# New durations in a hand-made order planner, vector products let through earlier, a conformer moved up: a two-layer hybrid diffusion backbone on one Trainium2 core

## The chip, the cores and the metric

One core of a Trainium2 chip runs the whole program. The metric is device time in microseconds, the median of three runs. A core has five engines with a queue of their own each: TensorE (PE) multiplies matrices, VectorE (DVE) and ScalarE (ACT) work on rows, GpSimd (POOL) does some additions, SyncE (SP) issues the DMAs. Each takes its instructions in the order in which the program puts them, and waits at semaphores for the others.

## The reference

Two layers over 256 latent and 256 context tokens of width 1024. In each layer a modulated RMSNorm feeds one wide projection, whose columns go to four mixers; their outputs are projected, gated, summed and projected again; then sixteen experts choose their tokens.

```python
for l in range(2):
    mod = silu(c) @ ada_w[l] + ada_b[l]                  # shifts, scales, gates (also for the context)
    u = modulate(rms_norm(h), mod[0], mod[1])
    z = u @ w_in[l]                                      # diff q,k,v | hyena | conformer | mla q,kv | 4 gates
    y = [diff_attention(z), hyena(z), conformer(z), mla(z)]
    h = h + mod[2] * ((sum(sigmoid(g[i]) * (y[i] @ w_branch[i]) for i in range(4))) @ w_out)
    h = h + mod[5] * expert_choice_ffn(modulate(rms_norm(h), mod[3], mod[4]))   # 16 experts, 32 tokens each
return rms_norm(h_latent)
```

In the second layer only the latent tokens are carried to the end; the context serves as keys and values. Everything is float32; the large products are made from a high and a low part (three matmuls each, `mm3`, lines 355 to 357).

## The kernel before

The program is straight-line: its order on every engine is fixed when it is built. Each piece of work is a Python generator (a worker) that emits instructions and yields what they cost: `{"pe": ..., "dve": ..., "act": ...}`. `Order.run` (line 175) keeps one planned clock per engine. It goes through the list of workers and resumes the first whose ready time is not after the planned TensorE time; if none is ready, the one that is ready soonest, and TensorE's planned time moves there. So the place in the list is the priority. The costs of the row engines come from `_a`, `_d` and `_q` (lines 215 to 225), those of TensorE from constants at the place (0.00042 us a column of a matmul). The planner knows nothing of the PSUM buffers (two `pm`, three `psc`, two `pt`, one `px`); the real waits for them come on the chip.

Layer 0's list begins with the experts' loader, the router and `head`, which cuts the weights of the wide projection into high and low parts (`wq`, ScalarE's cast in line 348, the vector's subtraction in line 349). Then come the modulation products. `body` (line 910), the matmuls of the wide projection, is last: it fills TensorE when nothing else is ready, in pieces of twelve matmuls of 512 columns in layer 0 (256 in layer 1). Its last items are the gates of the four branches, in the order 1, 3, 2, 0 (hyena, latent attention, conformer, differential attention); in layer 0 at most four gate results (`tg`) may be outstanding (`TGMAX`, line 921), in layer 1 ten. `branch` (line 998) multiplies a mixer's output by its weights and by the gate.

The products (`half`, line 500) compute the later shifts, scales and gates on VectorE: a job is one load of 256 KB by SP and, per stream (two in layer 0, one in layer 1), a scalar_tensor_tensor with accumulation (line 521). 96 jobs run in layer 0 and 64 in layer 1. After a job the worker waits until the planned end of its vector work plus `PACE[l]`. When a group is through, a closing worker (`end`) spreads the result as rows (POOL copies, transposes); the first group's are needed by the output projection, which in layer 0 also waits for all products.

The conformer (line 1218) runs 31 taps for each of two halves on VectorE (line 1230), in pairs, then a layer norm through transposes (its last steps are in lines 1260 to 1262). `CP` gives its place: -1 is just above `body`. The latent attention (`mla`, 16 steps in layer 0, 8 in layer 1) and the differential attention (`diff`, as many) go step by step: scores on TensorE, maximum (line 1272) and its negative (1274) on VectorE, exponential (1276) on ScalarE, scaling, transposes, and the product with the values; after a step they wait for the latest planned end plus `LAG[l]`. The differential attention's fourth step waits for the latent attention's end.

`S.wait` (line 249) makes the workers with the overall numbers 41 and 51 wait 0.7 us longer; before, these are the products' row loader of layer 1 and the conformer of layer 1.

```python
PACE, AHEAD = (0.0, -1.5), 2          # 236
CP, RLAG = (-1, -1), 4.0              # 238
S.wait = {41: -0.7, 51: -0.7}         # 249
e = yield {"dve": len(ss) * (_d(512) + 0.07)}   # 524
yield e + PACE[l]                               # 525
gens.insert(CP[l] if CP[l] >= 0 else len(gens) - 1, conformer())   # 1627
```

## Time and profile before

| | us |
|---|---|
| median of 3 runs | 1980.32 (1976.28 to 1982.57) |
| the profiled execution, its own time | 1979.82 |
| its span, first to last instruction | 1978.0 |
| TensorE busy | 1698.5 (86%), mean granted clock 0.913 |
| VectorE busy | 974.6 (49%) |
| ScalarE busy | 461.9 (23%) |
| POOL busy | 220.0 (11%) |
| read from HBM | 547.83 MB |

The span falls into four parts: layer 0's mixers up to about 683 us, its experts up to 1129, layer 1's mixers up to 1514, its experts up to the end. The shares over the span mix these parts; the rows below are taken by stretch. A group of instructions is listed by its source line; `mm3` and `split` are helpers, so that lines 348, 349 and 355 to 357 are told apart by the tiles they write and read. Matmuls are pipelined and their ends are modelled, so a matmul's duration in the trace is longer than the distance between two starts.

### The profile page before, as it was taken

Reading aid. Unit: us, or ns where it says so; the run is one execution under the profiler, and the core shown is the slowest. Engines: PE = TensorE matmul, PEld = TensorE weight load, DVE = VectorE, ACT = ScalarE, POOL = GpSimd, SP = SyncE. Lnnn points to the kernel's source line nnn. Section 1 sums busy time; section 2 is a strip of 40 time slices with the busy share of each in tenths; the row PEclk is TensorE's granted clock in tenths of the full one; section 3 lists DMA queues with packets and bytes.
Section 4 is the critical chain, followed back from the end, with each engine's and each line's share of the span. In section 5 each row is a group of like instructions: output and inputs, shape, how many; then the busy total and the mean of one; then the engine's idle time right before and its main releaser. Section 6 shows DMA issues by size and latency. Waiting matters only on the chain.

```text
span 1978.0 us, 27907 instructions
## 1 busy us (share of the span) xinstructions
PE 1698.5 (86%) x11132; PEld 1106.7 (56%) x11132; DVE 974.6 (49%) x2057; ACT 461.9 (23%) x933; POOL 220.0 (11%) x229
## 2 busy tenths in 40 slices
PE   5899999888989899899999888998997776676675
PEld 2677788666769634433333278887997433322222
DVE  4787789877774312212332285888864111111012
ACT  4423233334332100100100063344442000000001
POOL 1332011031101000000010042320211000000000
PEclk9899999899989899989999998999998877778677
DMA  8525334422345799999999954565759999999997
GB/s 284 170 86 169 128 114 139 145 95 85 111 151 215 267 375 417 419 408 420 419 418 421 404 180 142 172 197 161 220 176 362 417 421 420 420 421 420 421 421 304
DMA packets 185721, 550.71 MB, mean 278 GB/s; under 512 B 13238, under 2 KB 93304, under 8 KB 140408
## 3 DMA queue, kind: packets, MB, share of 16 engines
q1 hardware_dynamic: 185592, 548.94, 72.9%
q8 instruction: 88, 1.44, 0.3%
q14 instruction: 41, 0.34, 0.1%
HBM read 547.83 MB, written 1.05 MB: 277 GB/s over the span
## 4 chain that ended last, share of the span: by engine, by line
PE 50%; DMA 26%; DVE 12%; issue 6%; ACT 4%; POOL 1%; SPq 1%; ACTq 0%; DVEq 0%; POOLq 0%
DMA we<-in_w_ei_dram 14%; PE pm L1965 11%; DMA we<-in_w_eo_dram 9%; PE pm L355 7%; PE pm L357 7%; PE pm L356 7%; PE psc L1990 4%; DVE wq L349 2%; PE psc L1854 2%; PE psc L355 2%; PE psc L357 2%; DVE aw L521 1%; PE psc L356 1%; DMA aw<-in_ada_w_dram 1%; ACT wq L348 1%
## 5 line engine op out<-in xcount | busy, mean ns | idle before, releaser
L1965 PE MATMUL pm<-we,xe 128*32 128x256 f32 (+1 forms) x3040 | 419.4, 543 | 91.0 <-DMA we<-in_w_ei_dram 89.2
L1965 PEld LDWEIGHTS pm<-we,xe 128*32 128x32 f32 (+1 forms) x3040 | 142.1, 137 | 344.6 <-issue 188.6
L355 PE MATMUL pm<-uh,wq 128*128 128x256 f32 (+1 forms) x832 | 291.3, 350 | 2.2 <-ACT u L819 1.9
L356 PE MATMUL pm<-ul,wq 128*128 128x256 f32 (+1 forms) x832 | 281.6, 338 | 1.0 <-POOL ul L828 1.0
L357 PE MATMUL pm<-uh,wq 128*128 128x256 f32 (+1 forms) x832 | 281.3, 338 | 0.0
L1977 DVE SCALAR_TENSOR_TENSOR ea<-ea,pm 128x512 f32<-128x512 f32 (+1 forms) x32 | 17.7, 553 | 420.9 <-ACT ea L1976 420.9
L1990 PE MATMUL psc<-we,eaT 128*32 128x256 f32 (+1 forms) x1440 | 185.2, 509 | 36.7 <-DMA we<-in_w_eo_dram 35.7
L349 DVE TENSOR_TENSOR wq<-wi,wq 128x1024 fp32r<-128x1024 f32 x131 | 166.9, 1285 | 80.3 <-ACT wq L348 79.9
L355 PEld LDWEIGHTS pm<-uh,wq 128*128 128x128 f32 x832 | 161.3, 194 | 23.9 <-issue 5.2
L356 PEld LDWEIGHTS pm<-ul,wq 128*128 128x128 f32 x832 | 161.5, 194 | 17.6 <-POOL ul L828 1.2
L357 PEld LDWEIGHTS pm<-uh,wq 128*128 128x128 f32 x832 | 160.9, 193 | 16.6
L2002 DVE TENSOR_TENSOR ye<-psc,modr 32x512 f32<-32x512 f32 (+1 forms) x120 | 66.4, 553 | 197.0 <-PE psc L1990 195.7
L1990 PEld LDWEIGHTS psc<-we,eaT 128*32 128x32 f32 (+1 forms) x1440 | 64.5, 129 | 151.8 <-issue 81.6
L348 ACT CAST wq<-wi 128x1024 fp32r<-128x1024 f32 x132 | 136.2, 1044 | 11.8 <-DMA wi<-in_w_in_dram 10.4
L1976 ACT ACTIVATE ea<-pm 128x512 f32<-128x512 f32 (+1 forms) x32 | 15.7, 491 | 473.2 <-PE pm L1965 473.2
L1230 DVE SCALAR_TENSOR_TENSOR ca<-up,colt,ca 128x510 f32<-128x510 f32 (+29 forms) x120 | 81.0, 675 | 2.2
L521 DVE SCALAR_TENSOR_TENSOR aw<-aw,h 128x512 f32<-128x512 f32 x96 | 77.5, 807 | 3.4
L2035 ACT COPY eaT<-pt 128x512 f32<-128x512 f32 (+1 forms) x32 | 15.3, 479 | 273.1 <-PE pt L2033 273.1
L1276 ACT ACTIVATE e<-psc,nm 128x512 f32<-128x512 f32 (+1 forms) x72 | 44.4, 617 | 147.7 <-DVE nm L1274 142.8
L355 PE MATMUL pm<-wq,uh 128*128 128x256 f32 (+1 forms) x240 | 72.4, 302 | 4.4 <-DVE rsq L319 1.6
L356 PE MATMUL pm<-wq,uh 128*128 128x256 f32 (+1 forms) x240 | 70.3, 293 | 0.0
L357 PE MATMUL pm<-wq,ul 128*128 128x256 f32 (+1 forms) x240 | 70.2, 293 | 0.0
(407 smaller groups left out, 2603.1 us busy)
## 6 DMA issues: line engine op xcount, KB each, us to landing
we<-in_w_ei_dram SPq DMA_DIRECT2D x241, 1024.0 KB, 19.7
we<-in_w_eo_dram SPq DMA_DIRECT2D x120, 1024.0 KB, 19.8
wi<-in_w_in_dram SPq DMA_DIRECT2D x58, 1024.0 KB, 5.3
aw<-in_ada_t_dram SPq DMA_DIRECT2D x160, 256.0 KB, 5.4
we<-in_w_ei_dram SPq DMA_DIRECT2D x52, 256.0 KB, 8.1
wbr<-in_w_branch_dram SPq DMA_DIRECT2D x40, 256.0 KB, 5.4
wi<-in_w_out_dram SPq DMA_DIRECT2D x8, 1024.0 KB, 5.1
we<-in_w_eo_dram SPq DMA_DIRECT2D x32, 256.0 KB, 5.4
```

Of the source, the lines that this page charges most:

```text
L348: nc.scalar.copy(hi, src)
L349: eng.tensor_tensor(lo, src, hi.bitcast(F32), op=OP.subtract)
L355: nc.tensor.matmul(out, lh, rh, start=first and i == 0, stop=False)
L356: nc.tensor.matmul(out, lh, rl, start=False, stop=False)
L357: nc.tensor.matmul(out, ll, rh, start=False, stop=last and i == n - 1)
L521: nc.vector.scalar_tensor_tensor(o, wt_, 1.0, cb[s, k], op0=OP.mult, op1=OP.mult, accum_out=ends[lm, g][0][:, s, c, k:k + 1])
L1230: nc.vector.scalar_tensor_tensor(o, up[:, :, max(d, 0):256 + min(d, 0)], cw[:, c0 + d:c0 + d + 1], o, op0=OP.mult, op1=OP.add)
L1276: nc.scalar.activation(e, p[:, :nk], AF.Exp, scale=scale, bias=nm, accum_out=s)
L1854: nc.tensor.matmul(p[:, kk * n:(kk + 1) * n], h[2 * s + b][k // 4][:, (k % 4) * 128:(k % 4 + 1) * 128], hot[:, 2 * i + b], start=b == 0, s ...
L1965: nc.tensor.matmul(dst[j * M:(j + 1) * M, :], lhs, w[o + j * FW // 512][:, j * FW % 512:j * FW % 512 + FW], start=k == 0, stop=k == KC - 1 ...
L1990: nc.tensor.matmul(py[j * M:(j + 1) * M, :FW], aT[:, c * 128 + q * M:c * 128 + (q + 1) * M], w[f % 2 * 2 + j * FW // 512][:, j * FW % 512: ...
L2002: nc.vector.tensor_tensor(ye[eg][s][c0 // 512][e4 * CAP:(e4 + 1) * CAP, c0 % 512:c0 % 512 + FW], py[r0:r0 + CAP, :FW], mod5[r0:r0 + CAP, c ...
```

## The change

The planner's constants are replaced: a matmul column 0.000442 us instead of 0.00042, the vector 0.13 + n/915 instead of 0.07 + n/960, POOL 0.15 + n/450 instead of 0.1 + n/480, and 0.1 us (`HOP`) is added to the end of each engine's part of a step before the next engine's part starts. `PACE` of layer 0 goes from 0.0 to -1.5, the value of layer 1. `CP` of layer 1 goes from -1 to 5: the conformer is sixth in layer 1's list of mixers, behind the key rotation and ahead of the products, the query rotation, the differential attention and the branches. All numbers of workers behind it in the list rise by one.

```diff
@@ Order.run
                     e = self.t[k] = max(self.t[k], e) + c
+                    e += HOP
                 best[3] = e
...
+HOP = 0.1
...
 def _d(n):
-    return 0.07 + n / 960
+    return 0.13 + n / 915
 def _q(n):
-    return 0.1 + n / 480
+    return 0.15 + n / 450
...
-    PACE, AHEAD = (0.0, -1.5), 2
+    PACE, AHEAD = (-1.5, -1.5), 2
     PRE, PREW = (1, 3), (1, 3)
-    CP, RLAG = (-1, -1), 4.0
+    CP, RLAG = (-1, 5), 4.0
...
-                                        yield {"pe": 3 * PIECE[l] * step * 0.00042}
+                                        yield {"pe": 3 * PIECE[l] * step * 0.000442}
...
-                            e = yield {"pe": 24 * 0.00042 * w, **cost}
+                            e = yield {"pe": 24 * 0.000442 * w, **cost}
...
-                        e = yield {"pe": 24 * 0.108, "dve": _d(256), "dve " if q == 3 else "pool": _d(256)}
+                        e = yield {"pe": 24 * 0.119, "dve": _d(256), "dve " if q == 3 else "pool": _d(256)}
...
-                    PE = {"pe": nk * 3 * TQ * 0.00042, "dve": _d(TQ)}
+                    PE = {"pe": nk * 3 * TQ * 0.000442, "dve": _d(TQ)}
...
-            MF = 12 * 0.213 * F
+            MF = 12 * 0.226 * F
```

## Rows read from the trace of the kernel before

**Rows 1.** Busy time by stretch: engine, us busy (instructions); clock; DMA share; GB/s.

```profile
core 0: us, PE busy (x) PEld busy (x) DVE busy (x) ACT busy (x) POOL busy (x), PEclk, DMA share, GB/s
...
100.00:216.00 116.00, 109.22 (x558) 88.45 (x557) 96.63 (x188) 32.86 (x61) 26.52 (x24) 0.96 0.37 120
216.00:374.00 158.00, 157.35 (x860) 128.92 (x859) 132.39 (x303) 56.75 (x118) 15.78 (x16) 1.00 0.41 131
374.00:557.00 183.00, 154.05 (x717) 118.40 (x715) 139.92 (x314) 65.56 (x136) 37.46 (x36) 0.92 0.37 119
...
683.00:1129.00 446.00, 422.57 (x1944) 162.56 (x1946) 114.61 (x204) 37.60 (x74) 6.93 (x9) 0.97 1.00 409
...
1160.00:1255.00 95.00, 85.72 (x604) 79.31 (x603) 68.50 (x143) 39.89 (x82) 29.19 (x34) 0.93 0.49 157
...
1300.00:1374.00 74.00, 69.36 (x533) 61.65 (x531) 61.73 (x142) 36.05 (x76) 4.18 (x3) 0.98 0.59 185
1374.00:1452.00 78.00, 74.20 (x604) 73.38 (x604) 59.46 (x111) 37.10 (x64) 15.77 (x18) 0.98 0.60 190
...
1540.00:1965.00 425.00, 295.35 (x3136) 124.64 (x3128) 58.11 (x137) 16.61 (x45) 0.00 (x0) 0.76 1.01 417
```

**Rows 2.** Waits of TensorE, 374 to 609 us: us in total, times, longest.

```profile
PE psc L355 <- ACT wbrh L348: 11.2, 3, 6.7
PE psc L355 <- ACT e L1276: 8.5, 4, 6.2
PE pt L561 <- DVE ol L1522: 4.1, 1, 4.1
```

**Rows 3.** Timeline near 479 us: start, us, instruction, [idle before it, what ended it].

```profile
479.12 0.69 ACT L1276 ACTIVATE e<-psc,nm 128x512 f32<-128x512 f32 x1 [1.26 <-DVE nm L1274]
...
479.95 0.80 PE L355 MATMUL psc<-oh,wbrh 128*128 128x512 f32 x1 [6.24 <-ACT e L1276]
```

**Rows 4.** Line 1418, layer 0: duration ns min/median/max, first and last start.

```profile
L1418 PE MATMUL px<-aT,mv x96: 272/273/324, 251.3 to 368.1; 128*64 128x128 f32 x96
```

**Rows 5.** Timeline: matmuls in a full run, and after a wait.

```profile
480.55 0.63 PE L356 MATMUL psc<-ol,wbrh 128*128 128x512 f32 x1
...
480.97 0.63 PE L357 MATMUL psc<-oh,wbrl 128*128 128x512 f32 x1
...
544.67 0.39 PE L357 MATMUL pm<-uh,wq 128*128 128x512 f32 x1
...
548.75 0.39 PE L357 MATMUL pm<-uh,wq 128*128 128x512 f32 x1
```

**Rows 6.** VectorE's groups, 0 to 1140 us: count, busy us, mean ns, idle before.

```profile
L349 DVE TENSOR_TENSOR wq<-wi,wq 128x1024 fp32r<-128x1024 f32 x66 | 83.5, 1275 | 49.8 <-ACT wq L348 49.7
...
L1272 DVE TENSOR_REDUCE mx<-psc 128x1 f32<-128x512 f32 x24 | 16.4, 682 | 0.7 <-PE psc L1429 0.7
```

**Rows 7.** Line 521, the products, layer 0 and layer 1: ns, first and last start.

```profile
L521 DVE SCALAR_TENSOR_TENSOR aw<-aw,h x96: 691/692/1683, 89.8 to 583.9; 128x512 f32<-128x512 f32 x96
...
L521 DVE SCALAR_TENSOR_TENSOR aw<-aw,cb x64: 674/683/1219, 1175.4 to 1413.4; 128x512 f32<-128x512 f32 x64
```

**Rows 8.** Line 521's busy time in one stretch (products and their accumulator reads).

```profile
374.00:557.00 183.00, 50.19 (x125) 0.92 0.37 119
```

**Rows 9.** The conformer: taps in layer 0, last step in layer 0 and layer 1.

```profile
L1230 DVE SCALAR_TENSOR_TENSOR ca<-up,colt,ca x60: 715/732/1771, 121.8 to 383.8; 128x510 f32<-128x510 f32 x4, 128x508 f32<-128x508 f32 x4, 128x506 f32<-128x506 f32 x4, 128x504 f32<-128x504 f32 x4
...
L1262 DVE SCALAR_TENSOR_TENSOR cx<-cs,cx x2: 691/692/692, 453.6 to 456.5; 128x512 f32<-128x512 f32 x2
...
L1262 DVE SCALAR_TENSOR_TENSOR cx<-cs,cx x2: 424/438/452, 1447.5 to 1449.5; 128x256 f32<-128x256 f32 x2
```

**Rows 10.** Timeline near 421 us: two products and a POOL addition.

```profile
420.48 0.68 DVE L521 SCALAR_TENSOR_TENSOR aj<-aw,h 128x512 f32<-128x512 f32 x1
...
421.20 1.66 DVE L521 SCALAR_TENSOR_TENSOR aw<-aw,h 128x512 f32<-128x512 f32 x1
...
420.64 1.67 POOL L1056 TENSOR_TENSOR acc<-acc,tg 128x512 f32<-128x512 f32 x1 [0.29 <-DVE tg L1054]
```

More of the change, by code (lines that the diff above doesn't have):

```diff
@@ L933, in body @@
                                     if c + step < tn or k < KC - PIECE[l]:
-                                        yield {"pe": 3 * PIECE[l] * step * 0.00042}
+                                        yield {"pe": 3 * PIECE[l] * step * 0.000442}
                             done(j, m)
                             cost = fn(p[:, :tn], evs[m])
-                            e = yield {"pe": 3 * PIECE[l] * step * 0.00042, **cost}
+                            e = yield {"pe": 3 * PIECE[l] * step * 0.000442, **cost}
                             evs[m][0].t = e
```

## The prediction

> **What bounds the kernel now.** I read the busy time by stretch first [rows 1]. In the two expert stretches, 683 to 1129 us and 1540 to 1965 us, the DMA engines are busy the whole time (share 1.00 and 1.01, 409 and 417 GB/s): their length is the weights' transfer, and the order of the engines can't shorten it. They begin when the mixer before them ends, so what the change is worth is decided in the two mixers and passes on one for one. In the mixers TensorE is the engine that is short: from 216 to 374 it is busy 157.35 of 158 us, with VectorE at 132.39. From 374 to 557 that breaks down: TensorE is busy 154.05 of 183 us, so 29.0 us are idle, at a mean granted clock of 0.92, while VectorE is busy 139.92. This is the largest hole that ordering could fill; layer 1 has 9.3 us in 1160 to 1255, 4.6 us in 1300 to 1374 and 3.8 us in 1374 to 1452. The waits of TensorE in that stretch [rows 2] are led by the branch matmuls (line 355, psc<-oh,wbrh) that wait for ScalarE's cast of their weights, 11.2 us, and for ScalarE's exponentials, 8.5 us. Both are ScalarE standing behind VectorE: in the example of [rows 3] the exponential at 479.12 had waited 1.26 us for VectorE's maximum (line 1274), and TensorE's matmul at 479.95, which needs the PSUM tile that the exponential frees, had waited 6.24 us. So in layer 0 the end of the mixer is set by attention steps going round TensorE, VectorE and ScalarE, with the gate matmuls as filling: the four gate results that may be outstanding are used up while a branch waits. The latent attention's last products of the weights and values start at 368.1 us [rows 4], and the wait of 6.7 us in rows 2 follows it at once.
>
> **The change part by part.** No instruction is added or removed; matmuls, vector instructions and DMAs are those of before, in another order on each queue. So every cost is the cost of an order.
>
> Durations. Before, the planner charges a piece of twelve matmuls of 512 columns 12 x 512 x 0.00042 = 2.58 us; the trace has 18 starts between 544.67 and 548.75 us, 0.2267 us each, 2.72 us a piece [rows 5]; the new 0.000442 gives 2.72. A cut of 1024 columns on VectorE was 1.14 us, becomes 1.25, and takes 1.275; a maximum over 512 was 0.60, becomes 0.69, and takes 0.682 [rows 6]. So the plan's TensorE was 5% and its VectorE 11 to 13% too quick; VectorE's queue therefore fell behind what TensorE was told to expect. That is now largely gone, and 0.1 us is added after every step of an engine. What it buys can't be read from a row of its own. From above it can save what rows 2 hold; from below it can cost: a later predicted end moves an attention step behind one more piece of gate matmuls, 2.72 us each. I charge 2 us, between -3 us (a tenth of rows 2's sum) and +25 us (nine such steps).
>
> Products in layer 0 (line 525, 0.0 to -1.5). A product job is one load of 256 KB on SP's queue and two vector instructions with their accumulator reads. It was let through when the plan's VectorE had finished the last one; now 1.5 us before, about the length of a job in the new plan, 2 x (0.69 + 0.07) = 1.52 us. They stand third among layer 0's workers, ahead of attention, so they now keep VectorE's plan filled. They run until 583.9 us [rows 7], and in 374 to 557 take 50.19 us of VectorE [rows 8], 36% of its work there. VectorE is idle 19.4 + 25.6 = 45.0 us from 100 to 374 [rows 1]. I let half of that, 22 us, be filled by products from later: 22 / 50.19 = 44% of them leave the stretch with the waits. If TensorE's idle time there falls in proportion: 0.44 x 29.0 = -12.8 us (bounds 0 and -29). Clock: after such a wait matmuls start 0.42 us apart (480.55 to 480.97, rows 5) instead of 0.2267, that is 1.2 GHz for 2.4, some seven each time (an estimate from the few starts beside it), 7 x 0.2 = 1.4 us; the longest three of rows 2 exceed 4 us, and the 11.2 us of the first row's three hold a fourth, so 5.6 us, 44% of it -2.5 us. On the other side, 22 us more on VectorE in 100 to 374 (229 becomes 251 of 274 us) will make TensorE wait there, where it now idles 6.8 + 0.65 = 7.4 us; I take +5 us, two thirds of a doubling (bounds 0 and +15). On SP each of the 96 loads moves ahead of weight loads issued later, w_in's and the branches'; no wait of TensorE in rows 2 ends on a DMA, so I cost it at nothing, and up to +5 us if that cover goes.
>
> Conformer in layer 0. It stays last but one in the list, and products now press harder on VectorE above it. Its taps start from 121.8 to 383.8 us, its tail ends with the instruction started at 456.5 [rows 9], and its branch is the third of four. I take +2 us for its being late, bounds 0 and +30 (thirty pairs of taps, at most 1.5 us later each, less the slack ahead of its branch).
>
> Conformer in layer 1 (line 1627, -1 to 5). It moves from just above the filling matmuls to the place after the key rotation, ahead of the products and the diff attention. Its wait of 0.7 us belongs to list number 51 (line 249), and the moved conformer gets number 41, which has the same entry; so that holds, and the entry at 51 falls to the second closing step of the products, which nothing waits for at once. Its tail now ends at 1449.5 us [rows 9], with VectorE instructions, the POOL powers and two POOL subtractions; all of these move ahead on their queues, and the products (until 1413.4, rows 7) and their row copies on POOL move back. The products are needed for the output projection, some 70 us after that, so the delay is covered; if the cover went, every microsecond would count. The branch that uses the conformer could start sooner, but TensorE is busy 74.20 of 78 us there, so it can gain 3.8 us there, or lose as much in 1300 to 1374. I take -2 us, bounds -7 and +7.
>
> Start and expert stretches: 0, with 5 us either way for the start.
>
> One rule of the Trainium skill bears on where products go. In the trace a product takes 0.68 us at 420.48 and the next one 1.66 us, with a POOL addition of 1.67 us beginning at 420.64 [rows 10]. The Trainium skill's SBUF — State Buffer, section Who interferes with whom, says that a VectorE instruction with two SBUF inputs contends with a GpSimd instruction that reads SBUF. The trace agrees at this place. POOL is busy 26.52 of 116 us, 15.78 of 158 and 37.46 of 183 in the three stretches, so by that rule the moved products would become a little shorter, and the sum would be about 1 us lower than mine, which prices them as they are.
>
> **The sum.** -12.8 - 2.5 + 5 + 2 + 2 - 2 = -8.3 us. The profiled execution took 1979.82 us (span 1978.0); that gives 1971.5, and since its time lies within 0.5 us of the median of the runs (1980.32), I forecast 1971 us.
>
> **The rivals.** A, the forecast: products leave the stretch from 374 to 557 and part of its waits with them, 1962 to 1978 us. B, the whole hole closes: 29 + 5.6 us go, 1979.8 - 34.6 = 1945 us. For it: all of rows 2 ends on VectorE, or on ScalarE behind it. Against it: the vector stretches before have only 45 us of room.
>
> C, no difference: the waits come from the three PSUM tiles that attention and branches share (line 355's matmul waits for the exponential that reads one), and the planner counts no PSUM, before or after; another order then puts the same waits elsewhere, 1979 us. A sentence of the Trainium skill speaks for it: Perfetto Trace Analysis, Optimization Strategy, says that a gap repeating on the engine that should be saturated can mean too little SBUF or PSUM for the next tile; by that the time would stay. The 6.24 us wait of rows 3 fits it, the 4.1 us wait for line 1522 in rows 2 does not.
>
> D, slower: with products let through 1.5 us sooner, each maximum of an attention step in layer 0 finds up to one more product job ahead of it on VectorE, and the plan moves the step's next part behind one more piece, 2.72 us. TensorE has no room from 216 to 374, so it doesn't stall there: it does its filling sooner, meets the limit of four gates, and idles until the latent attention is through. Three such steps use up the 8.3 us; from the fourth on it is a loss. With eight of the sixteen steps: 1971.5 + 8 x 2.72 = 1993 us. For it: the products stand ahead of attention in the list, and the wait of 6.7 us comes just when that attention ends. Against it: pieces and steps now have their true length, which makes room for part of it.
>
> **How the numbers follow.** Chances: A 0.45, B 0.12, C 0.18, D 0.25. A measurement of this kernel tells about 0.3%, 6 us, from no change. Of A, 0.38 lies more than that below 1980 and 0.07 within; of C 0.16 within and 0.01 on each side; of D 0.23 above and 0.02 within. Faster: 0.12 + 0.38 + 0.01 = 0.51; within: 0.07 + 0.16 + 0.02 = 0.25; slower: 0.23 + 0.01 = 0.24. The range reaches from B's time to just beyond D's, 1945 to 1994; A alone would be 1960 to 1980.
>
> **What would show it.** Right: the last product starts well ahead of 583.9 us; TensorE's idle time in the stretch that answers to 374 to 557 falls from 29 to about 16 us at a higher granted clock; VectorE is busier from 100 to 374; layer 0's experts begin some 8 to 10 us sooner, and the expert stretches keep their length. In layer 1 the conformer's tail ends well ahead of 1449.5 and the output projection comes at most a few us sooner. Wrong: the latent attention's end lies later than 368 us with TensorE idle after it (D); products end sooner, but TensorE's waits have the same sum (C); a gain that comes from layer 1, or an expert stretch that changes its length.

## The result, and the profile after

The changed kernel takes 2037.4 us (median; 2036.6 to 2038.2) against 1982.1 us for the kernel before in the same comparison, a ratio of 1.0279 (95% interval 1.0266 to 1.0291). It is 55 us slower where 9 us faster was forecast, and lies outside the range. The profiled execution took 2036.67 us, its span is 2034.7 us, and its mean granted clock is 0.896 (0.913 before). All line numbers of the changed kernel are four higher than those of the kernel before.

First the cuts between the parts, from the router's first vector instruction (line 1826, now 1830) in each layer:

| us | before | after | difference |
|---|---|---|---|
| start to layer 0's router | 673.7 | 716.9 | +43.2 |
| layer 0's router to layer 1's router (experts 0, mixer 1) | 848.5 | 862.5 | +14.0 |
| layer 1's router to the end | 455.8 | 455.3 | -0.5 |

Next the busy time by stretch, with the stretches cut at the same work as in [rows 1] (engine, us busy and instructions; then clock, DMA share, GB/s):

```profile
core 0: us, PE busy (x) PEld busy (x) DVE busy (x) ACT busy (x) POOL busy (x), PEclk, DMA share, GB/s
100.00:230.00 130.00, 122.33 (x595) 99.78 (x593) 95.85 (x188) 35.10 (x65) 27.45 (x24) 0.91 0.35 114
230.00:392.00 162.00, 155.93 (x850) 127.61 (x848) 132.15 (x298) 59.14 (x121) 13.86 (x16) 0.99 0.38 123
392.00:600.00 208.00, 161.80 (x716) 123.91 (x716) 159.29 (x357) 63.37 (x131) 40.29 (x37) 0.87 0.35 113
...
726.00:1172.00 446.00, 422.73 (x1948) 162.64 (x1948) 114.65 (x204) 37.48 (x74) 6.91 (x9) 0.97 1.01 411
...
1600.00:2020.00 420.00, 291.27 (x3046) 121.47 (x3035) 56.76 (x135) 15.84 (x42) 0.00 (x0) 0.75 1.01 418
```

The expert stretches are what they were: DMA share 1.01 at 411 and 418 GB/s. The loss is in the mixers. The stretch that was to lose its hole, 374 to 557 us before, is now 392 to 600: TensorE idles 46.2 us in it instead of 29.0, and the clock is 0.87 instead of 0.92. Over the whole of layer 0's mixer, one row of the changed kernel and one of the kernel before carry the same 3148 matmuls:

```profile
0.00:717.00 717.00, 621.05 (x3148) 492.05 (x3148) 497.94 (x1076) 231.09 (x460) 116.52 (x121) 0.92 0.42 140
```

```profile
0.00:673.00 673.00, 599.50 (x3148) 476.19 (x3148) 494.31 (x1073) 230.13 (x460) 117.88 (x121) 0.95 0.45 149
```

So of these 44 us half are idle time (96.0 us against 73.5) and half are the same matmuls taking 21.6 us longer, at a mean clock of 0.92 instead of 0.95. VectorE's work is the same to within 4 us. (What the clock does with the idle time is taken up at the end.)

A third of layer 0's loss is there before the latent attention begins. Up to the first cut, the changed kernel and then the kernel before:

```profile
0.00:230.00 230.00, 196.35 (x883) 143.07 (x883) 152.52 (x305) 77.58 (x139) 50.70 (x51) 0.90 0.49 161
```

```profile
0.00:216.00 216.00, 181.02 (x874) 131.53 (x875) 158.46 (x310) 78.03 (x139) 51.41 (x51) 0.95 0.50 168
```

TensorE's idle time is about the same there (33.7 us against 35.0); the 14 us are matmul time, at a clock of 0.90 instead of 0.95 and for 883 matmuls instead of 874. From cut to cut the loss is 14, 4, 25 and 1 us.

TensorE's waits from 392 to 600 us (us in total, times, longest), which answer to [rows 2]:

```profile
PE psc L359 <- ACT wbrh L352: 14.2, 2, 7.9
PE psc L359 <- ACT e L1280: 7.7, 5, 3.5
PE pt L1262 <- DVE cn L1255: 7.7, 1, 7.7
PE px L1540 <- DVE ol L1428: 4.0, 1, 4.0
```

The same kinds lead as before, 11.2 and 8.5 us then, and the conformer's transposes (line 1262), which did not wait, are a new one. The single lines that answer to [rows 4] and [rows 7] (duration ns min/median/max, first and last start):

```profile
L1422 PE MATMUL px<-aT,mv x96: 272/273/324, 263.5 to 388.5; 128*64 128x128 f32 x96
...
L525 DVE SCALAR_TENSOR_TENSOR aw<-aw,h x96: 691/692/1657, 91.4 to 587.4; 128x512 f32<-128x512 f32 x96
L525 DVE SCALAR_TENSOR_TENSOR aw<-aw,cb x64: 674/684/1233, 1218.0 to 1521.6; 128x512 f32<-128x512 f32 x64
```

The latent attention's last products start at 388.5 us instead of 368.1. The modulation products of layer 0, which were to be through sooner, end at 587.4 instead of 583.9. Those of layer 1 end at 1521.6 instead of 1413.4, that is 108 us later, while they began 43 us later (1218.0 for 1175.4).

One wait shows how the idle time in layer 0 comes about. The timeline of the changed kernel near 400 us (start, us, engine, line, instruction; in brackets the idle time before it and what ended it):

```profile
395.25 0.69 DVE L525 SCALAR_TENSOR_TENSOR aj<-aw,cb 128x512 f32<-128x512 f32 x1 [2.56 <-DMA aw<-in_ada_t_dram]
...
395.98 0.69 DVE L525 SCALAR_TENSOR_TENSOR aw<-aw,h 128x512 f32<-128x512 f32 x1
...
396.60 1.49 DVE L1234 SCALAR_TENSOR_TENSOR ca<-up,colt,ca 128x490 f32<-128x490 f32 x2
398.00 0.68 DVE L525 SCALAR_TENSOR_TENSOR aj<-aw,h 128x512 f32<-128x512 f32 x1
...
399.35 0.42 DVE L1276 TENSOR_REDUCE mx<-psc 128x1 f32<-128x256 f32 x1
399.80 0.15 DVE L1278 TENSOR_SCALAR nm<-mx 128x1 f32<-128x1 f32 x1
...
400.05 0.47 ACT L1280 ACTIVATE e<-psc,nm 128x256 f32<-128x256 f32 x1 [10.99 <-DVE nm L1278]
...
402.32 0.60 ACT L352 CAST wbrh<-wbr 128x512 fp32r<-128x512 f32 x1
...
402.98 0.80 PE L359 MATMUL psc<-oh,wbrh 128*128 128x512 f32 x1 [7.86 <-ACT wbrh L352]
```

Read it from the end. TensorE stood 7.86 us for a cast of branch weights. The cast stood on ScalarE's queue behind an exponential that had waited 10.99 us for the negated maximum. The maximum stood on VectorE's queue behind products (line 525) and a pair of conformer taps, and the first of these products had waited 2.56 us for its own load. A load, VectorE, ScalarE and TensorE stand one behind the other in the order that the planner wrote, and at the head is work that the output projection needs, some 260 us later (its first residual sum starts at 655.6 us).

In layer 1 one wait stands out, 17.63 us of TensorE. SP's queue (its DMA issues), VectorE, ScalarE and TensorE there:

```profile
1498.28 3.81 SPq L1697 DMA_DIRECT2D we<-in_w_ei_dram  x5
1502.14 6.40 SPq L1695 DMA_DIRECT2D we<-in_w_ei_dram  x4
1510.70 0.33 SPq L287 DMA_DIRECT2D aw<-in_ada_t_dram  x1
1513.18 2.87 SPq L1011 DMA_DIRECT2D wbr<-in_w_branch_dram  x2
...
1521.56 0.69 DVE L525 SCALAR_TENSOR_TENSOR aw<-aw,cb 128x512 f32<-128x512 f32 x1 [13.60 <-DMA aw<-in_ada_t_dram]
...
1522.24 0.62 ACT L352 CAST wbrh<-wbr 128x512 fp32r<-128x512 f32 x1 [14.74 <-DMA wbr<-in_w_branch_dram]
...
1522.92 0.58 PE L359 MATMUL psc<-ohl,wbrh 128*128 128x256 f32 x1 [17.63 <-ACT wbrh L352]
```

Nine loads of expert weights (five of 1 MB, four of 256 KB) were issued ahead of the last product weights and the last two branch weights. Before, the last branch weights were issued by 1465 us and the experts' next loads from 1476 on. So the mixer waited for transfers that it does not need.

### The profile page after: what moved, and what is told of

The parts are those of the page before. It is cut to its first block, busy times and chain, and to the rows that moved or that the text cites. A ratio compares the mean times of both kernels' runs of the same rounds, so it can differ in the third digit from the quotient of the medians.

```text
span 2034.7 us, 27911 instructions
## 1 busy us (share of the span) xinstructions
PE 1721.9 (85%) x11132; PEld 1123.2 (55%) x11132; DVE 977.0 (48%) x2057; ACT 463.0 (23%) x933; POOL 222.7 (11%) x229
```

## The experiments

All runs in one table (the lines of kernels that start from the changed one are four higher, in h1 and i1 up to eleven); the ratio is to the kernel before in the same comparison, with its 95% interval. The columns behind it are starts in layer 0 (us): the latent attention's last output (line 1424), the differential attention's last scores, the conformer's last step, the end of the last product (the readout of its sum); then layer 0's router, and the time from there to layer 1's router. They come from one profiled execution each, whose time lies up to 6 us from the median, so differences of a few us in them say little.

| kernel | median us | ratio | latent | diff | conf. | prod. | router 0 | to router 1 |
|---|---|---|---|---|---|---|---|---|
| before | 1982.1 | 1 | 373 | 524 | 457 | 584 | 673.7 | 848.5 |
| changed | 2037.4 | 1.0279 [1.0266, 1.0291] | 392 | 561 | 503 | 588 | 716.9 | 862.5 |
| e1_durations | 2016.4 | 1.0167 [1.0132, 1.0202] | 388 | 537 | 470 | 648 | 710.5 | 849.9 |
| e2_pace | 1991.5 | 1.0048 [1.0033, 1.0063] | 386 | 541 | 470 | 518 | 685.7 | 850.1 |
| e3_conformer | 1986.0 | 1.0022 [1.0007, 1.0036] | 377 | 527 | 460 | 587 | 676.6 | 852.8 |
| e4_dur_pace | 2021.2 | 1.0199 [1.0166, 1.0232] | 394 | 560 | 502 | 587 | 715.8 | 847.8 |
| f1_hop | 1998.1 | 1.0074 [1.0053, 1.0096] | 385 | 538 | 469 | 621 | 686.7 | 852.4 |
| f2_vector | 2004.6 | 1.0111 [1.0082, 1.0139] | 372 | 524 | 457 | 634 | 697.8 | 851.1 |
| f3_tensor | 1990.2 | 1.0041 [1.0027, 1.0055] | 360 | 521 | 484 | 568 | 680.8 | 845.3 |
| f4_lag | 2024.2 | 1.0225 [1.0194, 1.0256] | 395 | 539 | 511 | 569 | 701.7 | 863.1 |
| g1_conf_layer0 | 2045.8 | 1.0322 [1.0296, 1.0348] | 397 | 575 | 486 | 602 | 723.4 | 860.0 |
| g2_conf_behind | 2041.5 | 1.0300 [1.0273, 1.0327] | 394 | 560 | 502 | 587 | 715.9 | 866.7 |
| g3_repaired | 2021.6 | 1.0202 [1.0175, 1.0228] | 388 | 562 | 508 | 605 | 716.3 | 846.9 |
| g4_tensor_conf | 1984.4 | 1.0010 [0.9995, 1.0026] | 367 | 522 | 406 | 599 | 677.6 | 845.9 |
| h1_loads | 2023.3 | 1.0212 [1.0191, 1.0233] | 393 | 558 | 500 | 585 | 714.0 | 848.0 |
| h2_prod_behind | 2000.6 | 1.0097 [1.0067, 1.0127] | 361 | 495 | 473 | 614 | 677.3 | 865.5 |
| h3_before_lag | 1973.3 | 0.9950 [0.9932, 0.9968] | 365 | 505 | 466 | 591 | 662.7 | 849.3 |
| h4_before_behind | 2009.4 | 1.0147 [1.0124, 1.0171] | 365 | 503 | 470 | 637 | 701.3 | 849.3 |
| i1_both | 1986.6 | 1.0035 [1.0021, 1.0050] | 363 | 497 | 475 | 617 | 679.4 | 848.9 |
| i2_both_lag | 1992.5 | 1.0059 [1.0039, 1.0078] | 351 | 481 | 468 | 620 | 683.6 | 850.2 |

**The parts alone.** Each of the three edits by itself, and the first two together.

e1_durations, the changed kernel with the two other edits undone:

```diff
-    PACE, AHEAD = (-1.5, -1.5), 2
+    PACE, AHEAD = (0.0, -1.5), 2
-    CP, RLAG = (-1, 5), 4.0
+    CP, RLAG = (-1, -1), 4.0
```

> The new durations and the 0.1 us per step alone; pace and conformer as before. Theory D (durations): the longer planned times move attention's steps and the conformer's tail behind more gate matmuls; layer 0's experts then begin near 727 us as in the changed kernel, layer 1 stays at its 385 us from experts' end to router, and the time is 1982 + 43 = 2025 us. Theory P (pace): the early products fill VectorE's queue ahead of attention and conformer, and durations matter little: 1982 us, experts of layer 0 near 683 us.

(In this and the next expectation D stands for the durations and P for the pace; the prediction's rival D is theory P here.)

Measured 2016.4 us, 1.67% slower: the durations, for which the sum has +2 us, cost 33 us by themselves (26 to 40), between the two expectations. The products end at 648 us, 63 us later than before.

e2_pace, the kernel before with the products let through sooner:

```diff
-    PACE, AHEAD = (0.0, -1.5), 2
+    PACE, AHEAD = (-1.5, -1.5), 2
```

> Products of layer 0 let through 1.5 us sooner, everything else as before. Theory D: 1982 us within 6, layer 0's experts near 683 us. Theory P: 2025 us, layer 0's experts near 727 us, the conformer's last step in layer 0 near 500 us instead of 456.5.

Measured 1991.5 us, 0.48% slower: 9 us, between the two expectations. Its lines for the latent attention's last products (matmuls) and for the modulation products, the time that the latter take in two stretches, and all engines in the second (the cuts lie at the work of 374 and 557 us before):

```profile
L1418 PE MATMUL px<-aT,mv x96: 272/273/324, 263.5 to 381.6; 128*64 128x128 f32 x96
...
L521 DVE SCALAR_TENSOR_TENSOR aw<-aw,h x96: 691/692/1667, 90.2 to 516.9; 128x512 f32<-128x512 f32 x96
...
100.00:387.00 287.00, 98.49 (x270) 0.97 0.41 132
387.00:574.00 187.00, 43.93 (x104) 0.92 0.34 110
...
387.00:574.00 187.00, 154.50 (x716) 119.38 (x715) 140.51 (x297) 65.95 (x135) 36.41 (x29) 0.92 0.34 110
```

This is the change on which rival D rests, without anything else. The products end sooner, as the prediction says, at 516.9 us instead of 583.9. They fill the first stretch (98.49 us of VectorE instead of 82.25, where the prediction has 22 us more) and leave the second only in part (43.93 us instead of 50.19, where it has 28). The waits did not leave with them: TensorE idles 32.5 us in the second stretch instead of 29.0, where the prediction has 16. The latent attention is late, as D says, 381.6 instead of 368.1 us, but not in the way that D says: its first product is late by 12.2 us already (263.5 for 251.3, [rows 4]), and its sixteen steps add 1.3 us. The lateness outweighs the products' gain.

e3_conformer, the kernel before with the conformer moved up in layer 1:

```diff
-    CP, RLAG = (-1, -1), 4.0
+    CP, RLAG = (-1, 5), 4.0
```

> The conformer sixth in layer 1's list, everything else as before. Both theories of layer 0: layer 0 unchanged, its experts near 683 us. If the 14 us of layer 1 come from this edit alone: 1982 + 14 = 1996 us, the last product of layer 1 after 1470 us instead of 1413, and a wait of TensorE for a branch weight's load of over 10 us late in the mixer. If they come from the durations: 1982 us.

Measured 1986.0 us, 0.22% slower: 4 us, inside the bounds of the step (-7 to +7), on the other side of zero than its -2. Layer 1's last product starts at 1461.7 us instead of 1413.4, but no wait for its load appears.

e4_dur_pace, the changed kernel without the conformer's move:

```diff
-    CP, RLAG = (-1, 5), 4.0
+    CP, RLAG = (-1, -1), 4.0
```

> The changed kernel with the conformer of layer 1 back at its old place: durations and pace together. If layer 0's 43 us and layer 1's 14 us are separate: 2037 - 14 = 2023 us, layer 0's experts near 727 us, layer 1's products through before its last gate. If the conformer's move in layer 1 mended something that the durations broke: above 2037 us.

Measured 2021.2 us. So the pace adds 5 us to the durations, which is within the noise of these two runs, and the conformer's move adds 16 us to both, though it costs 4 by itself. The three parts do not add, 33 + 9 + 4 = 46 us against 55, and it is the conformer's move that makes the difference.

**The durations taken apart.** Three kernels, each the one before with one kind of the new constants.

f1_hop:

```diff
                     e = self.t[k] = max(self.t[k], e) + c
+                    e += 0.1
```

> Of the durations, only the 0.1 us after each engine's part; all else as before. The durations together gave 2016 us, 34 over before. Theory S (steps): what counts is the planned length of an attention step, made of several engines' parts; the 0.1 us at each of them moves steps behind more gate matmuls, and most of the 34 us are here: about 2005 us, the latent attention's last output in layer 0 after 385 us instead of 373. Theory V (vector): what counts is the planned load of VectorE, which holds the products back; then 1982 us within 6.

f2_vector:

```diff
-    return 0.07 + n / 960
+    return 0.13 + n / 915
-    return 0.1 + n / 480
+    return 0.15 + n / 450
```

> Of the durations, only those of VectorE and POOL; all else as before. Theory V: the products of layer 0 are held back as in the durations alone, where they ended at 648 us and the output projection's first result stood at 648 us as well; so last product near 640 us and 2005 to 2015 us. Theory S: products somewhat later, but under 605 us, and 1982 to 1990 us.

f3_tensor, the TensorE constants at their places:

```diff
-    3 * PIECE[l] * step * 0.00042
+    3 * PIECE[l] * step * 0.000442
...
-            MF = 12 * 0.213 * F
+            MF = 12 * 0.226 * F
```

> Of the durations, only TensorE's; all else as before. Both theories: a slower planned TensorE gives the row engines more room in each planned piece, so attention steps need no more pieces and the products end sooner than 584 us: 1975 to 1985 us. Over 1990 us would say that any new order costs, whatever the constant.

Measured 1998.1, 2004.6 and 1990.2 us: 15, 22 and 8 us by the ratios. They act on different work. The 0.1 us between the parts of a step moves the attention (latent 373 to 385, differential 524 to 538) and the products (621). The longer VectorE times leave the attention where it was (372 and 524) and hold back only the products, 584 to 634. What that costs stands in f2's timeline:

```profile
628.59 0.69 DVE L521 SCALAR_TENSOR_TENSOR aj<-aw,cb 128x512 f32<-128x512 f32 x1 [11.89 <-DMA aw<-in_ada_t_dram]
...
633.35 1.28 SPq L1605 DMA_DIRECT2D h<-in_x_dram  x3
...
635.35 1.41 POOL L973 TENSOR_TENSOR h<-h,yo 128x256 f32<-128x256 f32 x2 [50.81 <-DVE yo L972]
...
636.13 0.69 PE L1756 MATMUL pt<-tat,h 128*128 128x128 f32 x2 [18.82 <-POOL h L973]
```

Until they end, the products in layer 0 keep part of their input rows in tiles of `h`, which are loaded anew from `x` after the last product (line 1605). The output projection's worker waits for that in the plan, so its VectorE step (line 972) stands behind the last product, the residual sum on POOL (line 973) behind that, and TensorE waits 18.82 us for the sum. Of these, VectorE itself waited 11.89 us for a product's load; i1, below, shows where such a load stands. The truer TensorE constants bring the attention sooner (360) and the conformer later (484), and cost 8 us.

**The pause and the conformer of layer 0.** f4_lag, the changed kernel with a shorter pause after each attention step of layer 0:

```diff
-    LAG = (2.0, 1.0)
+    LAG = (1.0, 1.0)
```

> The changed kernel with the pause after an attention step of layer 0 at 1.0 us instead of 2.0; durations, pace and conformer as changed. Theory S: the longer planned steps and the pause count the same wait twice; with a shorter pause the latent attention's last output goes back from 392 to about 375 us, the last scores of the differential attention from 561 to about 530, and 2037 becomes about 2010 us. Theory V: the steps are not what holds layer 0; 2037 us within 6, or slower because more TensorE waits for PSUM.

Measured 2024.2 us, 13 us less than the changed kernel, all of it in layer 0 (716.9 to 701.7): the differential attention is back at 539, the latent attention not (395).

g1_conf_layer0, the changed kernel with the conformer of layer 0 further up:

```diff
-    CP, RLAG = (-1, 5), 4.0
+    CP, RLAG = (12, 5), 4.0
```

> The changed kernel with layer 0's conformer thirteenth in its list, ahead of the differential attention, instead of just above the filling matmuls. Theory H (held by the conformer): its last step at 503 us is what the third branch waits for, and with it the four gates and all after; with the conformer some 40 us sooner layer 0's router comes 10 to 20 us sooner and the time is 2017 to 2027 us. Theory S (steps): the differential attention, whose last scores stand at 561 us, holds layer 0 by itself, and taps ahead of it make it later: 2037 us or more.

Measured 2045.8 us, 8 us more. The conformer comes 17 us sooner (486), and the differential attention 14 us later (575): the conformer's lateness is not the cause, it is one of the ways in which VectorE's queue can be shared out.

g3_repaired, both of these and the conformer of layer 1 back in its old place:

```diff
-    CP, RLAG = (-1, 5), 4.0
+    CP, RLAG = (12, -1), 4.0
-    LAG = (2.0, 1.0)
+    LAG = (1.0, 1.0)
```

> The changed kernel with three settings taken back or moved: layer 0's conformer ahead of the differential attention, layer 1's at its old place, layer 0's pause after a step 1.0 us instead of 2.0. Theory H and S together: the three repairs (13 us for the pause, 16 for layer 1, 10 to 20 for layer 0's conformer) add up, 1988 to 1998 us, near the kernel before. If they mend the same wait: about 2010 us.

Measured 2021.6 us, above both expectations: in layer 0 the gain of the shorter pause is gone again (716.3). g4_tensor_conf, f3 with the conformer of layer 0 moved up:

```diff
-    CP, RLAG = (-1, -1), 4.0
+    CP, RLAG = (12, -1), 4.0
```

> The kernel before with TensorE's new durations alone, and layer 0's conformer ahead of the differential attention. With TensorE's durations alone the attention of layer 0 was sooner (last output 360 us for 373, last scores 521 for 524), but the conformer later (484 for 457). Theory H: with the conformer sooner the third branch starts sooner and the time falls below both kernels, 1970 to 1978 us. Otherwise 1984 to 1990 us.

Measured 1984.4 us, no difference to the kernel before: the TensorE constants alone cost nothing once the conformer, which they had delayed, has an earlier place. What this place does at the old constants was not tried.

**The products' place in layer 0.** h2_prod_behind, the changed kernel with layer 0's products behind the differential attention in the list:

```diff
-    BA, MS, MVP = (1, 1), (0, 1), (1, 5)
+    BA, MS, MVP = (1, 1), (0, 1), (11, 5)
```

> The changed kernel with layer 0's products behind the differential attention in the list of workers instead of just behind the wide projection's cuts. If the products' place ahead of attention is what makes attention late (theory D), the latent attention's last products of weights and values start near 373 instead of 392 and the last differential scores near 525 instead of 561; the output projection then hangs on the products' own end, which I expect at 600 to 640 against 588, so the time would be 2015 to 2030 us against 2037. If attention is late because of the planner's longer durations alone (theory S), it stays at 385 or later and 538 or later, the products end later still, and the time is 2040 to 2070.

Measured 2000.6 us, 37 us less than the changed kernel and better than the expectation. Its busy time up to the router, its latent attention, and the longest wait of TensorE from 560 to 700 us:

```profile
0.00:677.00 677.00, 602.50 (x3148) 479.31 (x3148) 494.97 (x1074) 231.61 (x460) 115.11 (x121) 0.95 0.45 148
...
L1422 PE MATMUL px<-aT,mv x96: 272/273/324, 248.4 to 356.6; 128*64 128x128 f32 x96
...
PE pt L1760 <- POOL h L977: 11.2, 1, 11.2
```

With the same durations and the same pace the latent attention ends at 356.6 us instead of 388.5, idle time is 74.5 us instead of 96.0, and the clock is back at 0.95. So it is the products' place ahead of attention that makes attention late; the durations alone don't do it. The price is the products' end at 614, which TensorE awaits for 11.2 us (a load has part in it, see i1).

h4_before_behind is the same edit in the kernel before:

> The kernel before with layer 0's products behind the differential attention in the list. Theory D says that the products' place ahead of attention already costs something before: the latent attention would end ahead of 368 and the differential scores ahead of 524, the products later than 584, and the time would be within 10 us of 1980 on either side, by which of the two the output projection waits for. If the products only take what VectorE leaves over, their place changes nothing: 1978 to 1984. If they starve, they end near 640 and the time is 2000 us or more.

Measured 2009.4 us, 1.47% slower. There too attention comes sooner (365 and 503), but the products, each let through only when the plan's VectorE is done, end at 637, and the same wait is

```profile
PE pt L1756 <- POOL h L973: 30.0, 1, 30.0
```

Within this wait VectorE waited 11.0 us for a product's load. So place and pace belong together: at the old durations the old pace is the better one ahead of attention (1982 against 1991.5), and it starves the products behind it.

**The loads in layer 1.** g2_conf_behind, the changed kernel with layer 1's conformer behind its products in the list:

```diff
-    CP, RLAG = (-1, 5), 4.0
+    CP, RLAG = (-1, 7), 4.0
```

> The changed kernel with layer 1's conformer eighth, behind the products, instead of sixth; still ahead of query rotation, differential attention and branches. If it is the products' delay that costs in layer 1 (last one at 1522 us, its loads and two branch weights behind expert weights on SP's queue): last product of layer 1 before 1490 us, no TensorE wait over 10 us for a branch weight, and 2037 - 16 = 2021 us as with the old place. If the place ahead of attention and branches is what costs: 2037 us within 6.

Measured 2041.5 us: the products end at 1529 all the same, and the wait for branch weights is 13.6 us. It isn't the conformer ahead of the products in the list that matters.

h1_loads, the changed kernel with one more condition for layer 1's experts' loader (`br_ev` is set when branches 0 and 2 have both issued their last weights, `aw_ev` when the last product's weights are issued):

```diff
-                if i == 0 and d2 == 2:
-                    br_ev.t = 0.0
+                if i in (0, 2) and d2 == 2:
+                    br_seen.add(i)
+                    if l == 0 and i == 0 or len(br_seen) == 2:
+                        br_ev.t = 0.0
...
                         yield br_ev
+                        if l == 1:
+                            yield aw_ev
```

> The changed kernel, with one more condition for layer 1's expert loads: the loader goes on only when the conformer's branch has issued its last weights and the products' last weights have been issued. No instruction is added or removed, only SP's queue has another order. In the changed kernel nine loads of 1 MB stand on that queue ahead of the last branch weights and the last product weights, and TensorE waits 17.6 us at 1522.9. Theory Q (queue): that wait is what the conformer's new place costs; it goes, layer 1's router comes 12 to 17 us sooner, and the time is 2020 to 2026 us, that is about what the same kernel takes with the conformer left behind (2021). Rival P (products): the products are late on VectorE anyway, their end stays near 1520 and the output projection with it; the time stays 2035 to 2040. Between them: the expert weights, asked for later, leave the DMA engines idle before the experts, and the gain in the mixer is given back in the experts.

(The nine loads are five of 1 MB and four of 256 KB, 6 MB in all, not nine of 1 MB.) Measured 2023.3 us, 14 us less. SP's queue now:

```profile
1494.68 3.17 SPq L287 DMA_DIRECT2D aw<-in_ada_t_dram  x2
1497.95 0.89 SPq L1014 DMA_DIRECT2D wbr<-in_w_branch_dram  x2
1498.89 2.89 SPq L1704 DMA_DIRECT2D we<-in_w_ei_dram  x5
1502.14 4.38 SPq L1702 DMA_DIRECT2D we<-in_w_ei_dram  x4
```

The expert loads start 0.6 us later than in the changed kernel (1498.89 against 1498.28), the two groups of small loads pass in front of them, and the longest wait for branch weights falls from 17.6 to 2.7 us. Layer 1's part of the loss (14.0 us) is gone, 848.0 us from router to router, and the experts lost nothing. The Trainium skill, DMA: Bandwidth & Descriptors, section Two DMAs through the same engine are not ordered, says that the descriptors within one queue of a DMA engine start in order. The trace agrees: the product weights issued at 1510.70 us behind the expert loads were there 10.8 us later, where the median from issue to landing for such a load is 4.0 us in h1.

**Do the two causes make up the whole?** i1_both, h1 and h2 together; i2_both_lag, the same with the shorter pause:

```diff
-    BA, MS, MVP = (1, 1), (0, 1), (1, 5)
+    BA, MS, MVP = (1, 1), (0, 1), (11, 5)
```

```diff
-    LAG = (2.0, 1.0)
+    LAG = (1.0, 1.0)
```

> The changed kernel with both repairs: layer 0's products behind the differential attention in the list, and layer 1's expert loads behind the last branch and product weights on SP's queue. If the two causes are what the change costs, they add: 2037 - 37 (the products' place alone) - 14 (the loads alone) = 1986 us, 1980 to 1992, about the kernel before, with layer 0's router near 677 and layer 1's near 1525. If the two share a cause, the time stays above 1992.

> The same with layer 0's attention steps pausing 1.0 us instead of 2.0. The shorter pause gave 9 us in the kernel before and 13 us in the changed one: if it is the same gain here, 1972 to 1978 us, as good as the kernel before with the shorter pause (1973). If the products, now behind attention, take what it leaves, so that a quicker attention delays them and the output projection, the time is 1980 to 1992.

Measured 1986.6 us, as expected by adding (1986): with these two orders put right, all three edits together cost 7 us, 0.35%, instead of 55. The rest lies in layer 0's end (679.4 against 673.7), where the products' end holds up the residual. There i1 shows the order of layer 1 once more, for the new condition holds in layer 1 alone:

```profile
595.83 2.40 SPq L1704 DMA_DIRECT2D we<-in_w_ei_dram  x5
598.68 2.71 SPq L1702 DMA_DIRECT2D we<-in_w_ei_dram  x4
603.60 0.33 SPq L287 DMA_DIRECT2D aw<-in_ada_t_dram  x1
...
615.32 0.69 DVE L527 SCALAR_TENSOR_TENSOR aj<-aw,h 128x512 f32<-128x512 f32 x1 [9.77 <-DMA aw<-in_ada_t_dram]
```

The same 6 MB of expert weights stand ahead of the last product's load, VectorE waits 9.77 us for it, and TensorE's 11.3 us for the residual hang on that. The same wait for a load near layer 0's end is in e1 (9.6 us), f2 (11.9), h2 (9.6), h4 (11.0) and i2 (11.2), and neither in the kernel before nor in the changed one, whose products end ahead of these expert loads. The condition was not tried in layer 0, so what it gives back there is not shown.

The shorter pause loses 6 us here, 1992.5, just above the second expectation: the attention is another 12 us sooner (351), the products are not (620), and TensorE waits

```profile
PE pt L1767 <- POOL h L980: 20.9, 1, 20.9
```

where i1 waits 11.3.

**A version that beats both.** h3_before_lag, the kernel before with the shorter pause:

```diff
-    LAG = (2.0, 1.0)
+    LAG = (1.0, 1.0)
```

> The kernel before with layer 0's attention steps pausing 1.0 us instead of 2.0 us after the latest planned end. In the changed kernel the shorter pause gave 13 us. If the pause is a margin for a planner whose durations are too short, it is needed here, and the kernel gets slower: 1985 to 2000 us, with TensorE waiting for scaled weights and exponentials of the attention. If the pause is too long for either planner, the latent attention ends some us sooner than 368 and the time is 1968 to 1978 us. If other workers fill it, 1979 to 1985.

Measured 1973.3 us, ratio 0.9950 (0.9932 to 0.9968): 10 us faster than the kernel before, 64 us faster than the changed one. Its latent attention, and the stretch of the hole:

```profile
L1418 PE MATMUL px<-aT,mv x96: 272/273/324, 244.2 to 360.0; 128*64 128x128 f32 x96
...
374.00:557.00 183.00, 159.59 (x743) 124.29 (x742) 150.07 (x323) 65.79 (x135) 39.69 (x38) 0.94 0.35 111
```

TensorE idles 23.4 us there instead of 29.0 at a clock of 0.94 instead of 0.92. The stretch holds 743 matmuls instead of 717; up to the router, over the same 3148, idle time is 70.2 us (663 - 592.8) instead of 73.5, and the matmuls take 592.8 us instead of 599.5, at 0.97 instead of 0.95. So part of the gain for which the prediction looked to the products comes from the attention's own pause.

## Why the prediction was wrong, point by point

**What bounds the kernel.** Right: the expert stretches kept their length and all the loss is in the mixers. Right also that the hole comes from attention steps standing behind VectorE; the timeline near 400 us is the chain of [rows 3] with more in it.

**Durations, +2 us (bounds -3 to +25).** The largest mis-sized term: +33 us alone, beyond its upper bound. The step argued only from the plan being truer, and took the attention steps as the one thing that a longer plan could delay. It left out that each worker which waits for a planned end gets its turn later, the products above all: 96 jobs, each let through at the plan's VectorE end. In e1 that held the last product back 63 us, past the output projection, whose residual needs them. In the prediction the products' end had no room worked out in layer 0 at all: it was 28 us, from 584 to the first residual at 612, and f2 and e1 used it up; they then also met the experts' loads on SP's queue (11.9 and 9.6 us). In the changed kernel, with the new pace, the products end at 588 again, in time, and the same VectorE queue costs at the attention, as h2 shows.

**Products in layer 0, -12.8, -2.5 and +5 us.** The sign was wrong. The step said that half of VectorE's 45 idle us from 100 to 374 would be filled with products, which leave the stretch from 374 to 557 and take its waits with them. In the changed kernel not one was moved forward: line 525 is busy 81.75 us from 100 to 392, line 521 was 82.25 us from 100 to 374. In e2, where 16 us of them moved, TensorE's idle time in that stretch did not fall (32.5 us). With the longer durations the new pace only gave back what they took (648 to 588), and by itself (e2) it moved products and lost 9 us. VectorE's idle time there was not free room: with part of it filled in e2, the latent attention began 12.2 us later. The +5 us for TensorE's waits came out in size (13.7 us idle from 100 to 392, 7.4 before), though no product had moved there. The clock term went the other way: 21.6 us of the 44 are matmuls at a lower granted clock. Up to the first cut the changed kernel loses 14 us with no more idle time than before; the sum has 0 for the start (5 either way).

**Conformer in layer 0, +2 us (0 to +30).** It came 46 us later (502.9 for 456.5) and its transposes now wait 7.7 us; g1 shows that bringing it forward makes things worse, so no cost of its own can be put down to it.

**Conformer in layer 1, -2 us (-7 to +7).** Alone +4, inside; on top of the rest +16, and this is the step whose cover I named wrongly. "The products are needed for the output projection, some 70 us after that, so the delay is covered": the products came 66 us later against the start of layer 1, which used that cover up, and what then ended last was a load: with the branches' and products' last loads moved back, the experts' loads, released by another branch's progress, passed them on SP's queue. With the conformer's move alone (e3) the products were 46 us late against the start of layer 1 and no load passed them, hence 4 us there and 16 here. The prediction looked at SP's queue for layer 0 alone and found no wait for a DMA there; for layer 1 it did not list what is queued behind the moved loads. h1 shows it.

**The rivals.** D was right in direction, and in naming the products' place ahead of attention, which h2 shows. Its mechanism is borne out only in part. Attention's last products came 20.4 us later, near D's eight pieces of 2.72 us, but that is luck: its first ones came 12.2 us later already (263.5 for 251.3), which leaves 8.2 us, three pieces, for its steps; in e2 it is 1.3 us. And D gave the delay to the pace, while the durations alone (e1) make the attention as late as the pace alone (388 and 386 for 373). The limit of four gates is in no run. D's price was too low because it held nothing for the clock, for the conformer's transposes and for layer 1. C, the PSUM tiles: with the same tiles and another order (h2) the idle time falls back from 96.0 to 74.5 us, so the bubbles follow the order here; the sentence on consistent bubbles of Perfetto Trace Analysis, Optimization Strategy, in the Trainium skill does not decide this case. Whether more tiles would help was not tried. The SBUF rule of the prediction could not show anything, since the products stayed where they were.

**The range.** Its upper end, 1994 us, took one mechanism at a time. The bounds of the steps added up (+25, +5 and +15, +30, +7) reach beyond 2037; e1 alone lies above the range.

**What stays open.** Why the three kinds of constants cost 45 us singly and 33 together; which of the waits cost the clock (below); what the expert loads' place costs at the end of layer 0 in i1; and what the pace with the products behind attention is worth at the old durations, which was not tried.

## What to carry to other kernels

In a list scheduler of this kind the durations are part of the tuning: truer durations with the old pauses, places and paces cost 33 us. Work that is needed late and stands ahead, in an in-order queue, of the short steps that feed the bounding engine delays them, however idle that queue's engine looks. Place and pace go together: ahead of these steps a slow pace (the fastest kernel here, h3, is of this kind), behind them a quick one. When a worker moves, list the DMAs that move with it and what on their queue is released by another event: one 6 MB prefetch in front of a 256 KB load cost 14 us.

## What the hardware showed that was not expected

The clock made up half of the loss in layer 0, and it does not follow the idle time by its sum. Up to the router the same 3148 matmuls were busy 621.1 us with 96.0 us idle among them in the changed kernel (clock 0.92), 602.5 us with 74.5 us idle in h2 (0.95), but in f2 only

```profile
0.00:698.00 698.00, 602.03 (x3148) 479.96 (x3148) 500.61 (x1076) 231.39 (x460) 114.48 (x121) 0.93 0.43 144
```

that is 602.0 us with as many idle us, 96.0, of which 18.8 are one wait near the end. The changed kernel's waits lie earlier and are spread: its clock is 0.91 from 100 to 230 us and 0.87 from 392 to 600. One long wait near the end does not explain f2, though: e1 has 95.6 us idle, 16.5 of them in such a wait, and its matmuls took 615.4 us. At the same sum of idle time the busy time thus differed by up to 19 us; which of the waits cost the clock no run here separates.
